# The last quarter of a weight slab's split: from GpSimd to VectorE, in every stage

## The chip, the cores and the metric

One core of one Trainium2 chip runs the whole program. The metric is device microseconds of one execution; the figure that counts is the median over several executions. The engines are named as the profile names them: PE is TensorE (PEld its weight loads), DVE is VectorE, ACT is ScalarE, POOL is GpSimd, SP is SyncE, which here issues nearly all DMAs.

## The reference, cut to what matters

256 tokens of width 1024 go through two stacks of blocks, all in float32. The first stack has two layers, each a swiglu feed forward, a mixed attention (three kinds of heads, one of them with a top-64 choice of keys by an indexer) and a second swiglu. The second stack has four layers, each a mixer (mamba2, hgrn2, gated deltanet, mamba2), a cross attention to a memory, and a convolutional glu:

```python
def swiglu(h, w1, w3, w2):
    return (jax.nn.silu(h @ w1) * (h @ w3)) @ w2
...
for i in range(DEPTH_2):
    hn = rmsnorm_2(x, ln_mix[i])
    mix = mamba2_mixer(...) | hgrn2_mixer(...) | gated_deltanet_mixer(...)
    x = x + mix
    x = x + memory_cross_attention(rmsnorm_2(x, ln_xattn[i]), rmsnorm_2(mem, ln_mem[i]), ...)
    x = x + conv_glu_ffn(rmsnorm_2(x, ln_ffn[i]), ...)
```

Every projection `h @ w` is a float32 product with some hundred tokens against a weight that is used once. The gated deltanet also solves 32 small triangular systems.

## The kernel before, in words

Weights come in slabs of 128 partitions by 2048 float32 values (1 MB, one DMA of SP each). `slab` splits a slab into a high and a low part so that three fast matmuls (high by high, high by low, low by high) give float32 accuracy: ACT writes the high part (`hi`, a rounded copy, L262), and a second engine the low part (`lo = src - hi`, L263). Tiles are named `w` (the slab as loaded, three buffers) and `wp` (its two parts, three buffers). `self.pieces` says into how many pieces the split is cut: 2 of 1024 columns in the feed forwards, 4 of 512 columns in the mixers, in the attention and in the first two steps of a swiglu. `self.share` says how many of the last pieces have their low part made by POOL in place of DVE: 1 of 4 in those stages, 3 of 4 in the triangular solve of the deltanet (`gsolve`), 0 elsewhere.

`up_block` multiplies a slab with the activations. It takes the eight contraction blocks k in turn for the slab's first 128 output columns and then again for the second 128, with three matmuls for each, 48 in all; a quarter piece of 512 columns holds two blocks k. A block of 24 matmuls so needs all four pieces. Results lie in a bank of PSUM (`up`, two of them; `acc`, four), and DVE takes them out and scales them (`scale`, L608).

Program order sets priorities: a framework's scheduler orders each engine's queue from the order in which the code records instructions and from its own idea of when each is ready. On PE the order is chained by hand (`chained`), so it is fixed. All queues run strictly in order.

In the mamba mixer a layer has 8 groups. A group takes three slabs: x (evacuated as `mps`, convolved into `mx`), B and C (evacuated as `mps` from an `acc` bank, convolved into `mbc`), and z (evacuated as `mz`). The convolutions are six fused multiply-adds of DVE each (L2016), `mm` are the decay matrices (exponentials of ACT, then times `ms` on DVE, L1430), which PE multiplies with `mxd`. POOL has other work there: masks (L1401), `mx` times a column (L1428), `my` times `mz` (L1443), a sum of squares (L1446). In the attention DVE picks the top 64 keys by repeated MAX and MATCH_REPLACE on `isc`. In `gsolve` the triangular systems are solved in 31 steps of two dependent operations each (`gyt`, a product, L1888, and `gy`, a subtraction, L1893); DVE has the columns from 20 on, POOL the columns below, while slabs of the value projection (`gpr` evacuated, `gv` convolved) go on beside it. POOL's first operation of each step is kept behind the last split that POOL was given (`self.shared`).

Of the kernel before, what the change touches and what calls it, by code (L numbers as in the profile page):

```python
# [188 lines left out]
class Net:  # L189
    def __init__(self, tc, a, out):  # L190
        self.tc, self.nc, self.a, self.out = tc, tc.nc, a, out
        self.es = ExitStack()
        pool = lambda name, bufs, **k: self.es.enter_context(tc.tile_pool(name=name, bufs=bufs, **k))
        self.cp = pool("const", 1)
        self.wp = pool("wf", 3)
        self.sp = pool("ws", 3)
        self.hp = pool("act", 1)
        self.tp = None
        self.ps = pool("ps", 2, space=PSUM)
        self.dp = pool("dram", 1, space=bass.MemoryType.DRAM)  # L200
        self.side = []
        self.pieces, self.share, self.first, self.r0 = 2, 0, False, None
        self.chain, self.linked, self.urgent, self.ready, self.beside = False, None, None, None, None
        self.shared = None
        self.table, self.used, self.loaded = None, [], None
        self.slabs, self.normed = 3, None
        self.n = 0
# [57 lines left out]
    def slab(self, src, n=2048):  # L265

        if self.ready is not None:
            parts, self.ready = self.ready, None
            return parts
        w = self.t([P, 2048], "w", pool=self.wp)[:, :n]  # L270
        if not self.first:
            self.nc.sync.dma_start(w, src)
        hi, lo = (v[:, :n] for v in self.parts([P, 2048], "w", pool=self.sp, at=0))
        m = n // self.pieces
        for k in range(0, n, m):
            if self.first:
                self.nc.sync.dma_start(w[:, k : k + m], src[:, k : k + m])
            e = self.nc.gpsimd if n - k <= self.share * m else self.nc.vector
            s = self.split(w[:, k : k + m], hi[:, k : k + m], lo[:, k : k + m], e)
            if e is self.nc.gpsimd:  # L280
                self.shared = s[1]
            if self.slabs == 2:

                for x, y in zip(s, self.normed):
                    self.after(x, y)
        self.slabs += 1
        return hi, lo
# [414 lines left out]
    def swiglu(self, l, i):  # L702
        nc, a = self.nc, self.a
        h, e = self.norm_shift(*self.mod_cols(l, 2 * i))
        w1, w3 = a["w1"][l, i], a["w3"][l, i]

        def part(s, g):
            self.pieces, self.share = (4, 1) if s < 2 else (2, 0)
            s1 = self.t([P, 2, T], "s1")
            if s == 0:  # L710
                ps = [self.acc_bank() for _ in range(4)]
# [313 lines left out]
    def attention_heads(self, l, h, qkc):  # L1025
# [50 lines left out]
        for g, ks in (  # L1076
# [14 lines left out]
        ):  # L1091
            for k in ks:
                turns.setdefault(k, []).append(g)
        self.pieces, self.share = 4, 1
        with self.chained():
            for k in range(32):
                next(units[k // 2], None)
# [1 line left out]
                    next(g, None)  # L1099
                if k in (5, 8, 11, 26, 30)[: 5 - l]:  # L1100
                    self.run_side()
        self.pieces, self.share = 2, 0

# [175 lines left out]
    def mamba(self, i):  # L1281
# [6 lines left out]
            "sums": self.dp.tile([32, T], F32, name=self.name("mad")),  # L1288
        }
        d["yh"], d["yl"] = self.parts([P, 16, T], "my", 1)  # L1290
        self.pieces, self.share = 4, 1
        with self.chained():
            groups = [self.mamba_group(ia, g, n, d) for g in range(8)]
            steps = self.mamba_steps(ia, n, d)
# [19 lines left out]
                for g in turns.get(k, []):  # L1314
                    next(g, None)
            self.residual(acc)
        self.pieces, self.share = 2, 0

    def mamba_steps(self, ia, n, d):

# [140 lines left out]
    def hgrn(self, i):  # L1461
# [21 lines left out]
        zeroed = self.t([P, 4, 512], "hz", bufs=1)  # L1483
        nc.gpsimd.memset(zeroed, 0.0)
        yh, yl = self.parts([P, 8, T], "hyy", 1)
        self.pieces, self.share = 4, 1
        with self.chained():
            pairs = [self.hgrn_pair(p, n, lb, ln1, zeroed, yh, yl) for p in range(4)]

# [18 lines left out]
                for g in turns.get(k, []):  # L1508
                    next(g)
            self.residual(acc)  # L1510
        self.pieces, self.share = 2, 0

    def hgrn_project(self, src, n, tag, bufs):

# [145 lines left out]
    def gdn(self, i):  # L1660
# [14 lines left out]
        with self.chained(), self.phase("gvalues"):  # L1675
# [3 lines left out]
            values = [self.gdn_value(n, h, vt, z) for n in range(16)]  # L1679
            half = self.gdn_halves(keys, values)  # L1680
            with self.phase("gkeys"):
                self.share = 1
                gates = self.gdn_gates(h, d)
                turns = {1: [gates], 4: [gates], 5: [gates]}
                for n in range(0, 8, 2):
                    for k, g in ((6, n), (6, n + 1), (8, n), (9, n + 1)):
                        turns.setdefault(2 * n + k, []).append(keys[g])
                for k in range(22):
                    next(half)
                    for g in turns.get(k, []):  # L1690
                        next(g, None)
            self.share = 3
            with self.phase("gsolve"):
                for k, _ in enumerate(self.gdn_solve(d)):
                    if k % 2:
                        next(half)
                for _ in range(6):
                    next(half)
            self.share = 1
            with self.phase("gcombine"):  # L1700
                pool = self.tp
                groups = [self.gdn_combine(d, q, pool) for q in range(8)]
# [5 lines left out]
                with self.phase("gheads"):  # L1708
# [15 lines left out]
                                w = self.down_slab(a["gout"][0, n // 2])  # L1724
                            self.down_step(acc, w, n % 2, y[n], n == 0, n == 15, range(2 * q, 2 * q + 2))
                    self.residual(acc)
        self.pieces, self.share = 2, 0

    def gdn_halves(self, keys, values):

# [138 lines left out]
    def gdn_solve(self, d):  # L1869
# [12 lines left out]
        for j in range(31, 0, -1):  # L1882
            for k, (e, c0, c1) in enumerate(((nc.vector, max(j, cut), 32), (nc.gpsimd, j, cut))):
                n = c1 - c0
                if n > 0:
                    sh = [P, n, j]
                    m = self.t([P, 256], f"gyt{k}", bufs=1)[:, : n * j].rearrange("p (c r) -> p c r", c=n)
                    ins = e.tensor_tensor(  # L1888
                        m, u[:, j : j + 1, 0:j].to_broadcast(sh), y[:, c0:c1, j : j + 1].to_broadcast(sh), op=OP.mult
                    )  # L1890
                    if k:
                        self.after(ins, self.shared)
                    e.tensor_tensor(y[:, c0:c1, 0:j], y[:, c0:c1, 0:j], m, op=OP.subtract)  # L1893
            yield
        for b in blocks:
# [235 lines left out]
```

## Time and profile before

| | |
|---|---|
| median of 3 executions | 3231.4 us (3229.79 to 3231.53) |
| profiled execution, its own time | 3237.62 us |
| span of the trace in it | 3235.8 us |
| busy: PE, PEld | 3113.1 us (96%), 3009.9 us (93%) |
| busy: DVE, ACT, POOL | 2407.7 us (74%), 1871.9 us (58%), 616.2 us (19%) |

Times of the trace are microseconds from the span's start. A row of the timeline merges instructions of one kind that follow one another: start, length from the first start to the last end, engine, line, operation, tiles written and read, shape, count; in square brackets is how long the engine was idle before it and what ended that. The matmuls are pipelined, so PE's busy share says little of its pace.

### The profile page before, as it was taken

The numbers are of one execution on the slowest core, as the hardware profiler recorded it, in microseconds if no ns is written. First come the engines' busy times: TensorE is split into PE (matmuls) and PEld (weight loads), VectorE is DVE, ScalarE is ACT, GpSimd is POOL, SyncE is SP. The second block draws the span as 40 slices with busy tenths as digits, with TensorE's granted clock in tenths as the row PEclk, the third lists the DMA queues.
The fourth block names the chain that finished last, engine by engine and source line by source line (L and its number), as shares of the span: only waits on it lengthen the run. The fifth ranks groups of instructions, "written<-read, shape, count | busy, mean of one in ns | idle before, by whom it ended". The sixth has DMA issues, their size and how long they took to land. (4 is left out here: it accounts for less than half of the span.)

```text
span 3235.8 us, 63172 instructions
## 1 busy us (share of the span) xinstructions
PE 3113.1 (96%) x25866; PEld 3009.9 (93%) x25866; DVE 2407.7 (74%) x4122; ACT 1871.9 (58%) x3317; POOL 616.2 (19%) x522
## 2 busy tenths in 40 slices
PE   8999999999999999999999999998799999999998
PEld 8999889999988999889999999997799999889998
DVE  6778678778777846887767677688957766897766
ACT  5554565454466545775545665476466545776644
POOL 1000222010032201443001220025512000443100
PEclk9999999999999999999999999999899999999999
DMA  8888435758843555445455345544334555445453
GB/s 277 316 302 318 169 131 209 293 214 303 296 161 118 212 194 185 160 157 186 170 194 181 131 170 183 183 155 178 118 112 156 194 207 199 164 171 182 162 192 123
DMA packets 96754, 624.85 MB, mean 193 GB/s; under 512 B 10640, under 2 KB 14800, under 8 KB 25424
## 3 DMA queue, kind: packets, MB, share of 16 engines
q1 hardware_dynamic: 96464, 620.82, 54.2%
q8 instruction: 203, 3.33, 0.4%
q14 instruction: 87, 0.71, 0.1%
HBM read 607.08 MB, written 13.70 MB: 192 GB/s over the span
## 5 line engine op out<-in xcount | busy, mean ns | idle before, releaser
L298 PE MATMUL up<-hp,wp 128*128 128x256 f32 x12360 | 1495.5, 282 | 14.9 <-DVE gpr L608 8.1
L298 PEld LDWEIGHTS up<-hp,wp 128*128 128x128 f32 x12360 | 1464.2, 191 | 28.3 <-issue 10.4
L262 ACT ACTIVATE wp<-w 128x512 fp32r<-128x512 f32 (+3 forms) x1392 | 1034.6, 787 | 699.7 <-PE acc L298 227.6
L263 DVE TENSOR_TENSOR wp<-w,wp 128x512 fp32r<-128x512 f32 (+3 forms) x1195 | 1139.9, 984 | 387.4 <-ACT wp L262 375.8
L263 POOL TENSOR_TENSOR wp<-w,wp 128x512 fp32r<-128x512 f32 (+1 forms) x197 | 282.7, 1438 | 1389.1 <-ACT wp L262 1284.5
L298 PE MATMUL acc<-gp,wp 128*128 128x256 f32 x4224 | 502.2, 279 | 0.0
L298 PEld LDWEIGHTS acc<-gp,wp 128*128 128x128 f32 x4224 | 494.7, 189 | 0.2
L455 DVE SCALAR_TENSOR_TENSOR w<-w,silu_c 128x512 f32<-128x512 f32 x288 | 191.2, 714 | 41.5 <-DMA w<-ada 41.3
L520 POOL TENSOR_TENSOR nss<-nss,nsq 128x512 f32<-128x512 f32 x38 | 52.8, 1389 | 557.3 <-ACT nsq L507 555.8
L298 PE MATMUL up<-wp,hp 128*128 128x256 f32 (+1 forms) x1056 | 145.1, 293 | 6.0 <-ACT hp L262 4.3
L298 PEld LDWEIGHTS up<-wp,hp 128*128 128x128 f32 x1056 | 134.4, 196 | 12.7 <-ACT hp L262 5.9
L298 PE MATMUL up<-mh,wp 128*128 128x256 f32 x512 | 94.5, 292 | 11.8 <-ACT wp L262 7.8
L354 ACT ACTIVATE s<-up 128x512 f32<-128x512 f32 x40 | 23.9, 598 | 125.8 <-PE up L298 125.8
L298 PE MATMUL acc<-hp,wp 128*128 128x256 f32 x768 | 95.0, 280 | 0.0
L298 PEld LDWEIGHTS up<-mh,wp 128*128 128x128 f32 x512 | 81.9, 200 | 12.9 <-ACT wp L262 8.0
L298 PE MATMUL up<-wp,mh 128*128 128x256 f32 x512 | 91.3, 280 | 2.3 <-DVE wp L263 1.9
L298 PE MATMUL acc<-xop,wp 128*128 128x256 f32 x768 | 92.9, 279 | 0.0
L298 PE MATMUL acc<-myp,wp 128*128 128x256 f32 x768 | 92.1, 280 | 0.5 <-DVE my L1442 0.5
L350 ACT ACT_TABLE_LOAD x71 | 91.1, 1283 | 1.7 <-PEq L2121 0.7
L298 PEld LDWEIGHTS acc<-myp,wp 128*128 128x128 f32 x768 | 89.6, 188 | 1.8 <-DVE my L1442 0.7
L298 PEld LDWEIGHTS acc<-xop,wp 128*128 128x128 f32 x768 | 90.3, 188 | 0.0
L298 PEld LDWEIGHTS acc<-hp,wp 128*128 128x128 f32 x768 | 90.0, 188 | 0.0
(472 smaller groups left out, 3916.5 us busy)
## 6 DMA issues: line engine op xcount, KB each, us to landing
w<-w SPq DMA_DIRECT2D x132, 1024.0 KB, 5.2
w<-ada SPq DMA_DIRECT2D x72, 1024.0 KB, 5.0
w<-min SPq DMA_DIRECT2D x48, 1024.0 KB, 4.9
w<-fg SPq DMA_DIRECT2D x44, 1024.0 KB, 4.9
w<-fu SPq DMA_DIRECT2D x44, 1024.0 KB, 4.9
w<-fd SPq DMA_DIRECT2D x44, 1024.0 KB, 4.9
w<-gin SPq DMA_DIRECT2D x24, 1024.0 KB, 5.0
w<-xv SPq DMA_DIRECT2D x16, 1024.0 KB, 6.2
```

What stands on the lines that cost most here:

```text
L262: a = self.nc.scalar.activation(hi, src, AF.Copy)
L263: return a, (engine or self.nc.vector).tensor_tensor(lo, src, hi.bitcast(F32), op=OP.subtract)
L298: self.link(self.nc.tensor.matmul(out, lhsT=lhsT, rhs=rhs, start=start, stop=stop, skip_group_check=True))
L350: self.loaded = self.nc.scalar.preload_act_table_set(name)
L354: self.used.append(self.after(self.nc.scalar.activation(out, src, func, **k), self.loaded))
L455: ins = nc.vector.scalar_tensor_tensor(c, c, 1.0, self.silu_c[:, z * 512 : z * 512 + 512], op0=OP.mult, op1=OP.mult, accum_out=sums[:, s % ...
L520: nc.gpsimd.tensor_tensor(s, s, q, op=OP.add)
```

## The change

`share` and `shared` go away. Every low part of a weight slab is made by DVE; the pieces stay as they are, and so do ACT's high parts, the DMAs and PE's order. In the solve POOL's product is no longer ordered behind a split.

```diff
@@ slab
-            e = self.nc.gpsimd if n - k <= self.share * m else self.nc.vector
-            s = self.split(w[:, k : k + m], hi[:, k : k + m], lo[:, k : k + m], e)
-            if e is self.nc.gpsimd:
-                self.shared = s[1]
+            s = self.split(w[:, k : k + m], hi[:, k : k + m], lo[:, k : k + m])
@@ swiglu
-            self.pieces, self.share = (4, 1) if s < 2 else (2, 0)
+            self.pieces = 4 if s < 2 else 2
@@ attention, mamba, hgrn (each)
-        self.pieces, self.share = 4, 1
+        self.pieces = 4
...
-        self.pieces, self.share = 2, 0
+        self.pieces = 2
@@ gdn: keys, solve, combine
-                self.share = 1
-            self.share = 3
-            self.share = 1
@@ gdn_solve
-                    ins = e.tensor_tensor(
+                    e.tensor_tensor(
                         m, u[:, j : j + 1, 0:j].to_broadcast(sh), y[:, c0:c1, j : j + 1].to_broadcast(sh), op=OP.mult
                     )
-                    if k:
-                        self.after(ins, self.shared)
```

POOL has 197 instructions fewer and DVE 197 more; PE, ACT and SP have the same instructions. Queue rows below are line, operation, tile written and tiles read with their numbers, shape, count.

First place: DVE in a middle group of the second mamba layer, from one evacuation of B and C (`mps3370`) to the next evacuation of x (`mps3392`). Slab `wp3375` belongs to z (`mz3377`), `wp3390` to the following x, `wp3396` to the following B and C, and `wp3405` to the following z. Before:

```order
L608 TENSOR_TENSOR mps3370_33039<-acc3367_32980,nr3215_31569 128x512
L263 TENSOR_TENSOR wp3390_33168<-w3389_33166,wp3390_33168 128x512 x3
L2016 SCALAR_TENSOR_TENSOR mbc3371_33041<-mps3370_33039,cols_98,mbc3371_33041 128x255 x2
L2016 SCALAR_TENSOR_TENSOR mbc3371_33041<-mps3370_33039,cols_98,mbc3371_33041 128x254 x2
L2016 SCALAR_TENSOR_TENSOR mbc3371_33041<-mps3370_33039,cols_98,mbc3371_33041 128x253 x2
L263 TENSOR_TENSOR wp3396_33244<-w3395_33242,wp3396_33244 128x512 x3
L608 TENSOR_TENSOR mz3377_33116<-up3376_33067,nr3215_31569 128x512
L263 TENSOR_TENSOR wp3405_33331<-w3404_33329,wp3405_33331 128x512
L1442 TENSOR_TENSOR my3372_33050<-acc3373_33051,mx3333_32682 128x512
L263 TENSOR_TENSOR wp3405_33331<-w3404_33329,wp3405_33331 128x512 x2
L608 TENSOR_TENSOR mps3392_33226<-up3391_33177,nr3215_31569 128x512
```

The same stretch of DVE's queue after the change:

```order
L604 TENSOR_TENSOR mps3370_33039<-acc3367_32980,nr3215_31569 128x512
L262 TENSOR_TENSOR wp3375_33058<-w3374_33056,wp3375_33058 128x512 x2
L2007 SCALAR_TENSOR_TENSOR mbc3371_33041<-mps3370_33039,cols_98,mbc3371_33041 128x255 x2
L2007 SCALAR_TENSOR_TENSOR mbc3371_33041<-mps3370_33039,cols_98,mbc3371_33041 128x254 x2
L2007 SCALAR_TENSOR_TENSOR mbc3371_33041<-mps3370_33039,cols_98,mbc3371_33041 128x253 x2
L262 TENSOR_TENSOR wp3375_33058<-w3374_33056,wp3375_33058 128x512 x2
L262 TENSOR_TENSOR wp3390_33168<-w3389_33166,wp3390_33168 128x512 x4
L262 TENSOR_TENSOR wp3396_33244<-w3395_33242,wp3396_33244 128x512 x3
L604 TENSOR_TENSOR mz3377_33116<-up3376_33067,nr3215_31569 128x512
L1438 TENSOR_TENSOR my3372_33050<-acc3373_33051,mx3333_32682 128x512
L262 TENSOR_TENSOR wp3396_33244<-w3395_33242,wp3396_33244 128x512
L604 TENSOR_TENSOR mps3392_33226<-up3391_33177,nr3215_31569 128x512
```

The last two pieces of the slab for `mz3377` now stand behind the convolution `mbc3371`; before, that slab's pieces on DVE were done a group earlier (in the rows before, the slab that follows `mz3377` is the next z, `wp3405`) and its fourth was POOL's. Slabs 1577, 1607, 1637 and 1667 of the first mamba layer and 3375, 3405 and 3435 of the second have their last two pieces moved so, and slab 3345 its last one.

Second place: DVE in the attention of the first layer, at the top-64 choice. Slab `wp523` belongs to one of the attention's input projections. Before, from its third piece on DVE to the end of the choice (its fourth was POOL's):

```order
L263 TENSOR_TENSOR wp523_5167<-w522_5165,wp523_5167 128x512
L773 TENSOR_TENSOR ropeu493_5014<-qn475_4908,consts_1050 128x128
...
L884 MATCH_REPLACE isc425_4606<-m8521_5160,isc425_4606 128x256
L882 MAX m8530_5223<-isc425_4606 128x8
L882 MAX m8531_5224<-isc425_4606 128x8
L884 MATCH_REPLACE isc425_4606<-m8530_5223,isc425_4606 128x128
L884 MATCH_REPLACE isc425_4606<-m8531_5224,isc425_4606 128x256
L888 TENSOR_SCALAR selb346_4114<-isc425_4606 128x128
L888 TENSOR_SCALAR selb346_4114<-isc425_4606 128x256
```

After, the end of the same stretch:

```order
L880 MATCH_REPLACE isc425_4606<-m8521_5160,isc425_4606 128x256
L262 TENSOR_TENSOR wp523_5167<-w522_5165,wp523_5167 128x512
L878 MAX m8530_5223<-isc425_4606 128x8
L878 MAX m8531_5224<-isc425_4606 128x8
L880 MATCH_REPLACE isc425_4606<-m8530_5223,isc425_4606 128x128
L880 MATCH_REPLACE isc425_4606<-m8531_5224,isc425_4606 128x256
L884 TENSOR_SCALAR selb346_4114<-isc425_4606 128x128
L884 TENSOR_SCALAR selb346_4114<-isc425_4606 128x256
```

The fourth piece has come to stand 15 instructions behind the third, with four passes of the choice and the rotation of `qn` in between. The second layer's attention has the same with its slab 1184.

Third place: DVE in the triangular solve, a few of its 31 steps. After the change a split stands between many of the dependent pairs; between the first step and the transposes that end the solve there are 30 splits, 8 evacuations `gpr` and 24 convolution steps `gv`, where there were 5, 5 and 17:

```order
L1881 TENSOR_TENSOR gyt02576_25831<-gu2551_25651,gy2552_25652 128x192
L262 TENSOR_TENSOR wp2608_26028<-w2607_26026,wp2608_26028 128x512
L1884 TENSOR_TENSOR gy2552_25652<-gy2552_25652,gyt02576_25831 128x8x24
L262 TENSOR_TENSOR wp2608_26028<-w2607_26026,wp2608_26028 128x512
L1881 TENSOR_TENSOR gyt02577_25834<-gu2551_25651,gy2552_25652 128x207
L262 TENSOR_TENSOR wp2608_26028<-w2607_26026,wp2608_26028 128x512
```

The three splits in these rows were POOL's before.

## Rows read from the trace of the kernel before

**Rows 1.** The page's first part: busy us, share of the span, instructions.

```profile
PE 3113.1 (96%) x25866; PEld 3009.9 (93%) x25866; DVE 2407.7 (74%) x4122; ACT 1871.9 (58%) x3317; POOL 616.2 (19%) x522
```

**Rows 2.** Groups by line, first the page's: count, busy us, mean ns, idle before.

```profile
L263 POOL TENSOR_TENSOR wp<-w,wp 128x512 fp32r<-128x512 f32 (+1 forms) x197 | 282.7, 1438 | 1389.1 <-ACT wp L262 1284.5
...
L263 DVE TENSOR_TENSOR wp<-w,wp 128x512 fp32r<-128x512 f32 x606 | 458.8, 788 | 99.6 <-ACT wp L262 88.2 <-issue 8.0 <-PE up L298 1.8
...
L2016 DVE SCALAR_TENSOR_TENSOR s<-fgs,cols,s 128x255 f32<-128x255 f32 x88 | 38.7, 478 | 2.0 <-ACT s L2014 2.0
...
L2016 DVE SCALAR_TENSOR_TENSOR mbc<-mps,cols,mbc 128x255 f32<-128x255 f32 x32 | 27.4, 894 | 0.0
```

**Rows 3.** Windows: stretch, PE, PEld, DVE, ACT, POOL busy, granted clock, DMA.

```profile
324.00:570.00 246.00, 236.85 (x1771) 214.67 (x1770) 187.27 (x428) 153.98 (x341) 62.95 (x55) 0.98 0.48 171
...
1770.00:1900.00 130.00, 129.15 (x1101) 125.53 (x1101) 86.95 (x162) 83.79 (x157) 34.13 (x24) 1.00 0.44 156
...
2255.00:2323.00 68.00, 46.07 (x345) 44.59 (x343) 66.46 (x105) 24.89 (x55) 43.33 (x60) 0.89 0.34 121
...
2750.00:2960.00 210.00, 195.90 (x1579) 183.53 (x1578) 178.99 (x297) 154.24 (x299) 89.92 (x71) 0.97 0.46 161
```

**Rows 4.** Windows of line 263 alone: DVE busy (count), POOL busy (count).

```profile
324.00:570.00 246.00, 86.73 (x118) 32.12 (x23) 0.98 0.48 171
...
1770.00:1900.00 130.00, 46.06 (x62) 20.58 (x15) 1.00 0.44 156
...
2255.00:2323.00 68.00, 5.58 (x7) 28.46 (x21) 0.89 0.34 121
2750.00:2960.00 210.00, 72.94 (x101) 44.12 (x29) 0.97 0.46 161
```

**Rows 5.** Timeline of the triangular solve.

```profile
2267.13 1.31 POOL L263 TENSOR_TENSOR wp<-w,wp 128x512 fp32r<-128x512 f32 x1
2267.22 1.50 DVE L2016 SCALAR_TENSOR_TENSOR gv<-gpr,cols,gv 128x255 f32<-128x255 f32 x1
```

**Rows 6.** Timeline of one mamba group in the second layer: DVE, then POOL, then PE.

```profile
2853.60 1.93 DVE L1430 TENSOR_TENSOR mm<-mm,ms 128x384 f32<-128x384 f32 x4
...
2858.00 3.48 DVE L2016 SCALAR_TENSOR_TENSOR mbc<-mps,cols,mbc 128x255 f32<-128x255 f32 x6
2861.41 1.88 DVE L263 TENSOR_TENSOR wp<-w,wp 128x512 fp32r<-128x512 f32 x3
...
2869.51 0.69 DVE L608 TENSOR_TENSOR mps<-up,nr 128x512 f32<-128x512 f32 x1 [3.22 <-PE up L298]
2870.25 1.95 DVE L1455 SCALAR_TENSOR_TENSOR hy<-my,cols,rstd 128x256 f32<-128x256 f32 x2
...
2872.72 1.67 DVE L263 TENSOR_TENSOR myp<-hy,myp 128x256 fp32r<-128x256 f32 x2
2874.31 2.44 DVE L2016 SCALAR_TENSOR_TENSOR mx<-mps,cols,mx 128x255 f32<-128x255 f32 x6
2876.68 1.94 DVE L1430 TENSOR_TENSOR mm<-mm,ms 128x384 f32<-128x384 f32 x4
...
2858.12 1.51 POOL L263 TENSOR_TENSOR wp<-w,wp 128x512 fp32r<-128x512 f32 x1 [1.79 <-ACT wp L262]
...
2854.19 2.00 PE L298 MATMUL acc<-mm,mxd 128*64 128x256 f32 x8 [2.25 <-DVE mm L1430]
2856.13 6.44 PE L298 MATMUL up<-hp,wp 128*128 128x256 f32 x48
...
2863.74 5.74 PE L298 MATMUL up<-hp,wp 128*128 128x256 f32 x48
```

**Rows 7.** Timeline of the first attention, at the end of the top-64 choice.

```profile
442.53 1.29 POOL L263 TENSOR_TENSOR wp<-w,wp 128x512 fp32r<-128x512 f32 x1 [2.98 <-ACT wp L262]
...
447.46 2.99 PE L298 MATMUL up<-hp,wp 128*128 128x256 f32 x24
451.58 0.70 PE L298 MATMUL ms<-nsq,consts 128*128 128x256 f32 x2 [1.14 <-ACT nsq L984]
...
451.41 0.61 DVE L882 MAX8 m<-isc 128x8 f32<-128x128 f32 x2
```

More of the change, by code (lines that the diff above doesn't have):

```diff
@@ L201, in __init__ @@
         self.side = []
-        self.pieces, self.share, self.first, self.r0 = 2, 0, False, None
+        self.pieces, self.first, self.r0 = 2, False, None
         self.chain, self.linked, self.urgent, self.ready, self.beside = False, None, None, None, None
-        self.shared = None
         self.table, self.used, self.loaded = None, [], None
@@ L1290, in mamba @@
         d["yh"], d["yl"] = self.parts([P, 16, T], "my", 1)
-        self.pieces, self.share = 4, 1
+        self.pieces = 4
         with self.chained():
@@ L1316, in mamba @@
             self.residual(acc)
-        self.pieces, self.share = 2, 0
+        self.pieces = 2
     def mamba_steps(self, ia, n, d):
@@ L1485, in hgrn @@
         yh, yl = self.parts([P, 8, T], "hyy", 1)
-        self.pieces, self.share = 4, 1
+        self.pieces = 4
         with self.chained():
@@ L1510, in hgrn @@
             self.residual(acc)
-        self.pieces, self.share = 2, 0
+        self.pieces = 2
     def hgrn_project(self, src, n, tag, bufs):
@@ L1726, in gdn @@
                     self.residual(acc)
-        self.pieces, self.share = 2, 0
+        self.pieces = 2
     def gdn_halves(self, keys, values):
```

## The prediction

> **What bounds the kernel now.** The engine totals come first: PE is busy for 3113.1 us of the span, 96%, DVE for 74%, POOL for 19% [rows 1]. As a mean that leaves DVE 828 us of room, and 197 more splits look free. A mean over stages doesn't decide it, so the next view is the windows [rows 3], with the split's own line beside them [rows 4]. The reader is to see three kinds of stage. In hgrn2 PE is busy for 129.15 of 130 us and DVE for 87: whatever DVE gets there, PE has its next slab. In the solve it is the reverse: DVE 66.46 of 68 us, PE 46.07 for 345 matmuls at a granted clock of 0.89, so DVE sets the time. The attention (DVE 187.3 of 246, clock 0.98) and mamba (DVE 179 of 210, PE 196, clock 0.97) lie between: PE is the bound with gaps, and a gap is DVE being late at one place. One mamba gap stands in the timeline: PE waits 2.25 us for `mm` of DVE [rows 6].
>
> **What goes and what comes.** The order shows the move done in full: 197 splits fewer on POOL, 197 more on DVE, so that the change doing nothing is ruled out. On POOL they took 282.7 us at 1438 ns each, and POOL was mostly waiting for ACT's high part ahead of them [rows 2]; no stage had POOL as its bound, so this time is worth nothing by itself. On DVE a split's mean is 788 ns [rows 2], but three in a row take 1.88 us [rows 6]: 0.63 each, the next beginning before the last has ended. 197 × 0.63 = 124 us of work added to DVE at most (eleven of the moved pieces are smaller).
>
> **What DVE gets back.** The trace shows that a DVE instruction beside a POOL split can stand still. In the solve `gv` 128x255 began 0.09 us behind a POOL split and took 1.50 us, ending 0.19 us after the split's 2268.44 [rows 5]; the same shape takes 0.478 as a mean over 88 [rows 2]. That is 1.02 us for one hit. The convolution `mbc` has a mean of 894 ns where `s<-fgs`, the same operation and shape, has 478: 32 × 0.416 = 13.3 us, or 0.83 for each of the 16 mamba groups, and in the group shown `mbc` x6 took 3.48 against 2.44 for `mx` x6, with POOL's split at 2858.12 beside it [rows 2, 6]: 1.04 again. A split that meets DVE waiting, or a DVE operation that it doesn't disturb, gives back nothing. So a moved split costs DVE 0.63 and returns 0 to 1.04; DVE's time is even when 61 of 100 splits hit. Bounds for DVE's busy time: all hit, 124 − 205 = −81 us; none, +124. With DVE 74% busy as a mean and nearer 85 to 98% in mamba and the solve, where a hit is likeliest, I take about six hits in ten, so DVE's total stays about even. What is left is the order: the work that comes back is an average, the late piece is at a place.
>
> The Trainium skill says the same of the cause and more of the size (SBUF — State Buffer, section Who interferes with whom): a DVE instruction with two SBUF inputs contends with a GpSimd instruction that reads SBUF, and the second of them blocks fully until the first is done. The hit of [rows 5] agrees. Were every split to block DVE for its whole length, DVE would get back 283 us for 124 by that rule (an estimate, from the 282.7 of [rows 2]). [Rows 6] show 1.04 for a split of 1.51, so the sum goes by the rows.
>
> **Mamba, where order costs.** Before, the z slab's last piece was POOL's and early; DVE's three were done a group ahead. Now its last two stand behind `mbc` in the first `order` place, for seven slabs of the two layers, and in an eighth one piece does: 8 of 16 groups. Worked on the group shown [rows 6], counted from `mm` at 2853.60: `mm` 1.93, then an evacuation and two splits (0.6 + 1.26), so `mbc` begins at about 3.8. It now takes 2.44: 6.2. Two splits more end at 7.5. PE needs the last piece for 6 matmuls of the first half and then for the 24 of the second: 30 at 0.12 (5.74 us for 48) = 3.6, end at 11.1. In the trace `up` ended at 2862.57, which is 8.97 after `mm`. So z's block ends 2.1 later, and nothing in front of PE covers it, as PE's order is fixed. Some of it comes back in the same period of 23.08 us (`mm` at 2853.60 and 2876.68): the run from `mps` to the next `mm` lies on the path too (2869.51 to 2876.68), and at most one hit of 1.0 is in it; three splits fewer or more move in this period. I take 0.8 back: +1.3 × 8 = +10. The other eight groups keep their order and get about 0.2 each: −2. Mamba: +8. Bounds: if the returned hits count in full and the late pieces are covered, −1.04 × 16 = −17; if nothing comes back, 8 × 2.1 + 8 × 1.26 = +27.
>
> **Attention.** POOL had the fourth piece of the slab at 442.53 to 443.82, and `up` began at 447.46 [rows 7]. Now DVE has it after the MATCH_REPLACE that comes just before the last pair of MAX, at 451.41: ready at about 452.1. Of the first block 18 matmuls can be done by then, six are left, 0.7: 452.8. PE went on to `ms` at 451.58, since it waited there anyhow for ACT (1.14); so the loss is 1.2, and two layers have it: +2.4. For the other 44 of the 46 splits here DVE's idle quarter (59 of 246 us) is the cover; without it, 12 more us. Bounds 0 (the choice runs earlier by as much as its hits are gone) to +10 (the piece delays the choice and both blocks).
>
> **Solve.** DVE is full, so each split counts: 21 × 0.63 = +13 [rows 4]. Of POOL's 28.46 us of splits there, with DVE busy for 98% of the time, most hit: 0.75 × 21 × 1.03 = −16. Net −3. The pairs `gyt`, `gy` depend on each other, and a split between them fills the time between; POOL's half of the steps no longer waits for splits. Bounds 13 − 22 = −9 to +6 (a third of them hit).
>
> **The rest.** hgrn2, the keys, the feed forwards' first slabs: PE 129 of 130 us [rows 3], DVE with 43 us of room in 130 for 15 × 0.63 = 9: nothing. If that cover were gone, 9 us.
>
> **Sum.** +8 + 2.4 − 3 = about +8 on the profiled execution's 3237.6: 3245 to 3246. That execution lies 6.2 above the median, so in terms of the median 3231.4 + 8 = about **3240**.
>
> **Rivals.** (a) *DVE becomes faster where it counts.* The freed `mbc`, `mx`, `gv` act on the path in all 16 groups and in the solve, and the late pieces are covered: −17 − 3 − 1, so 3210. For it: `mbc` is 0.83 a group longer than it need be, and PE waits for `mm`. Against: z's last piece comes after `mbc` in half of the groups, whatever `mbc` takes. It decides if `mbc` begins 2 us earlier than I have it, which needs the hits of the stretch before it to be two, not one. By the Trainium skill's rule above, this is what should happen. (b) *No change.* The late pieces end up in waits that are there: DVE waits 3.22 for PE ahead of `mps` [rows 6], PE for ACT in the attention. The +10 halves, the −2 and −3 stay: 3231 to 3236. For it: PE is 96% busy and most changes off it vanish. Against: DVE's wait for PE is not PE's wait, and the order of PE is fixed. (c) *DVE is the new bound of mamba and the solve*, with hits fewer than 4 in 10: +27 + 6 + 5, so 3270. Against: `mbc`'s 894.
>
> **Chances.** Slower as forecast 0.40, (c) 0.06, (b) 0.33, (a) 0.21. A measurement of this kernel tells about 0.2%, 6.5 us, from no change. The forecast of +8 lies near that bound, so some of its chance lies within it and some of (b) above: slower 0.45, same 0.34, faster 0.21. The likeliest case's own range is 3234 to 3248. The range holds most of (a) and leaves (c)'s end out: 3215 to 3262.
>
> **What would show it.** Right: `mbc`'s mean falls from 894 to about 480, DVE's split from 788 to about 700; DVE's busy total stays within 40 us of 2408; in mamba PE's `up` of 48 that follows the `mm` product waits for DVE's line of the split, about 2 us, in eight groups, where it had no such wait; in the attention `up` of 24 before `ms` stretches from 2.99 to about 5; the solve's window stays within some 5 us of 68. Wrong: `mm` to `mm` in mamba falls below 23.08 (then (a) is right), DVE's busy total falls by over 60 (hits are the rule), or rises by over 80 (they were rare), or PE waits for DVE in hgrn2, which I hold covered.

## The result: 43 us faster

The changed kernel takes 3188.3 us (3183.95 to 3192.29, 4 runs) against 3231.5 (3229.79 to 3238.45): a ratio of 0.9862, with a 95% interval of 0.9826 to 0.9898. The forecast was 3240, and the range began at 3215. The profiled execution has a span of 3188.0 us, 47.8 less than that of before. The page's first part answers to [rows 1], the groups by line and shape to [rows 2]:

```profile
PE 3085.4 (97%) x25866; PEld 2983.9 (94%) x25866; DVE 2396.7 (75%) x4319; ACT 1872.3 (59%) x3317; POOL 348.8 (11%) x325
```

```profile
L262 DVE TENSOR_TENSOR wp<-w,wp 128x512 fp32r<-128x512 f32 x792 | 550.3, 730 | 91.0 <-ACT wp L261 88.1 <-PE up L294 1.8
...
L2007 DVE SCALAR_TENSOR_TENSOR mbc<-mps,cols,mbc 128x255 f32<-128x255 f32 x32 | 14.6, 485 | 0.0
```

DVE has 197 instructions more and is busy 11 us less. `mbc` has fallen from 894 to 485 ns, the split from 788 to 730. So the stalls that POOL's splits had caused gave back about what the splits cost.

The windows of [rows 3], between the same matmuls (PE's order is the same in both kernels, so the k-th matmul marks the same place), and the span with its mean granted clock:

```profile
325.50:563.80 238.30, 232.84 (x1772) 212.00 (x1772) 185.88 (x455) 154.13 (x341) 32.68 (x32) 0.99 0.50 178
...
2217.30:2296.20 78.90, 62.83 (x535) 61.22 (x533) 76.86 (x154) 39.58 (x88) 17.64 (x38) 0.91 0.42 145
2700.30:2905.40 205.10, 191.71 (x1579) 178.91 (x1578) 175.69 (x326) 154.74 (x299) 45.75 (x42) 1.00 0.46 165
```

```profile
core 0: 3188.0 us, clock 0.992
```

The attention has lost 7.8 us and the second mamba layer 5.0; the solve with its transposes, up to the matmul that stood at 2345 before, takes 78.9 us where it took 89.9. The granted clock of the whole is 0.992 where it was 0.984: about 104 us at the lower level before, 51 after (twice the missing part of the clock, times the span). A microsecond at half clock costs at most half a microsecond, so this is up to 26 us of the 47.8. It is more than the usual difference: the kernel before was granted 0.983 to 0.990 in its executions on record, 0.987 on average, which against 0.992 makes some 16 us.

What PE waited for in the second mamba layer, from the view of waits (us, times, longest), first before, then after:

```profile
PE acc L298 <- DVE mm L1430: 11.0, 7, 2.4
PE ms L319 <- DVE mdd L1333: 1.8, 1, 1.8
PE up L298 <- DVE mm L1430: 1.3, 1, 1.3
```

```profile
PE up L294 <- DVE wp L262: 10.1, 7, 1.9
PE acc L294 <- DVE mm L1426: 2.3, 5, 0.7
PE ms L315 <- DVE mdd L1329: 0.8, 1, 0.8
```

The late z pieces are there: the seven waits lie in four groups of the layer and come to 1.9 to 2.8 us a group, where about 2 was forecast. What was not forecast: 10.0 us of waits for `mm` went. All waits of the layer together hardly fell, from 14.1 to 13.2 us, and the groups did not fare alike. The first `mm` of the layer's first group and of its last, before and then after (the fourth group's stand at 2853.60 in [rows 6] and at 2795.62 below):

```profile
2783.07 0.56 DVE L1430 TENSOR_TENSOR mm<-mm,ms 128x384 f32<-128x384 f32 x1 [0.19 <-PE ms L298]
...
2945.08 1.93 DVE L1430 TENSOR_TENSOR mm<-mm,ms 128x384 f32<-128x384 f32 x4
```

```profile
2732.53 0.54 DVE L1426 TENSOR_TENSOR mm<-mm,ms 128x384 f32<-128x384 f32 x1
...
2890.09 1.93 DVE L1426 TENSOR_TENSOR mm<-mm,ms 128x384 f32<-128x384 f32 x4
```

The first three periods from `mm` to `mm` took 70.5 us before and take 63.1; the last four, those with a late piece, took 91.5 and take 94.5. In the first mamba layer it is 72.6 and 64.0, then 91.3 and 96.1. One group with a late piece in the timeline of the changed kernel, DVE and then PE, against [rows 6]:

```profile
2795.62 1.94 DVE L1426 TENSOR_TENSOR mm<-mm,ms 128x384 f32<-128x384 f32 x4
2797.48 0.68 DVE L604 TENSOR_TENSOR mps<-acc,nr 128x512 f32<-128x512 f32 x1
2798.08 1.28 DVE L262 TENSOR_TENSOR wp<-w,wp 128x512 fp32r<-128x512 f32 x2
2799.28 2.44 DVE L2007 SCALAR_TENSOR_TENSOR mbc<-mps,cols,mbc 128x255 f32<-128x255 f32 x6
2801.65 4.29 DVE L262 TENSOR_TENSOR wp<-w,wp 128x512 fp32r<-128x512 f32 x7
...
2796.22 1.33 PE L294 MATMUL acc<-mm,mxd 128*64 128x256 f32 x8 [0.65 <-DVE mm L1426]
2797.48 2.99 PE L294 MATMUL up<-hp,wp 128*128 128x256 f32 x20
2802.38 3.45 PE L294 MATMUL up<-hp,wp 128*128 128x256 f32 x28 [1.92 <-DVE wp L262]
```

`mbc` x6 takes 2.44 where it took 3.48, the z block waits 1.92 for its piece and ends at 2805.83, 10.2 after `mm` (11.1 was forecast, 9.0 before). But PE's wait for `mm` is 0.65 where it was 2.25. Ahead of the 2.25, two of the six `mx` had stood beside a split of POOL:

```profile
2849.15 2.28 DVE L2016 SCALAR_TENSOR_TENSOR mx<-mps,cols,mx 128x255 f32<-128x255 f32 x2
2848.91 1.47 POOL L263 TENSOR_TENSOR wp<-w,wp 128x512 fp32r<-128x512 f32 x1
```

In the changed kernel all six take 2.82. In the five groups of the layer where DVE has the same operations from `mps` to `mm` in both kernels, that way took 7.8 us on average and takes 6.2; half of the difference is in the operations, the other half is idle time that went too.

Behind that wait for `mm` the clock was lower as well. Windows of the kernel before, from the matmuls ahead of the wait, through those right behind it, to those after them; then of the changed kernel, through its wait for the z piece:

```profile
2849.70:2853.40 3.70, 2.25 (x20) 2.05 (x19) 3.70 (x8) 2.95 (x4) 1.45 (x2) 1.00 0.51 157
2854.20:2857.40 3.20, 3.20 (x14) 2.35 (x15) 3.20 (x6) 3.20 (x8) 1.27 (x1) 0.51 0.08 31
2858.00:2862.40 4.40, 4.40 (x41) 4.40 (x40) 4.40 (x9) 0.63 (x1) 1.51 (x1) 1.00 0.66 238
```

```profile
2796.20:2802.40 6.20, 4.12 (x29) 3.26 (x29) 6.20 (x14) 4.92 (x10) 0.00 (x0) 1.00 0.00 0
2802.40:2805.80 3.40, 3.40 (x29) 3.40 (x30) 3.40 (x6) 0.05 (x1) 0.00 (x0) 1.00 0.72 236
```

Behind the wait for `mm` the clock was granted at 0.51, the lower of the two levels (1.2 GHz), for some 3 us: 14 matmuls in 3.2 us where 41 follow in 4.4. In the changed kernel it stays at 1.00 through the wait for the piece. Not every wait is followed by a lower clock: three of the layer's eight waits for `mm` were, but a wait of 2.37 us at 2900.11 was not; in the changed kernel's first mamba layer one of the seven waits for the piece was.

In the solve, the same steps of before and after, DVE's columns at width 228:

```profile
2286.14 1.49 DVE L1888 TENSOR_TENSOR gyt<-gu,gy 128x228 f32<-128x228 f32 x1
2287.66 1.38 DVE L1893 TENSOR_TENSOR gy<-gy,gyt 128x228 f32<-128x228 f32 x1
```

```profile
2247.44 0.38 DVE L1881 TENSOR_TENSOR gyt<-gu,gy 128x228 f32<-128x228 f32 x1
2247.75 0.68 DVE L604 TENSOR_TENSOR gpr<-up,nr 128x512 f32<-128x512 f32 x1
2248.35 0.38 DVE L1884 TENSOR_TENSOR gy<-gy,gyt 128x228 f32<-128x228 f32 x1
```

1.49 and 1.38 have become 0.38 and 0.38, and an evacuation fits between.

### The profile page after: what moved, and what is told of

It reads as the page before. It is cut to its first block, busy times and chain, and to the rows that moved or that the text cites. A ratio compares the mean times of both kernels' runs of the same rounds, so it can differ in the third digit from the quotient of the medians.

```text
span 3188.0 us, 62851 instructions
## 1 busy us (share of the span) xinstructions
PE 3085.4 (97%) x25866; PEld 2983.9 (94%) x25866; DVE 2396.7 (75%) x4319; ACT 1872.3 (59%) x3317; POOL 348.8 (11%) x325
## 5 line engine op out<-in xcount | busy, mean ns | idle before, releaser
L262 DVE TENSOR_TENSOR wp<-w,wp 128x512 fp32r<-128x512 f32 (+3 forms) x1392 | 1232.1, 918 | 373.5 <-ACT wp L261 364.9
L294 PEld LDWEIGHTS up<-hp,wp 128*128 128x128 f32 x12360 | 1449.3, 189 | 51.6 <-DVE wp L262 37.3
L451 DVE SCALAR_TENSOR_TENSOR w<-w,silu_c 128x512 f32<-128x512 f32 x288 | 184.5, 690 | 48.0 <-DMA w<-ada 47.8
L294 PEld LDWEIGHTS up<-wp,hp 128*128 128x128 f32 x1056 | 131.8, 193 | 11.1 <-ACT hp L261 4.3
L294 PEld LDWEIGHTS up<-wp,mh 128*128 128x128 f32 x512 | 79.5, 191 | 7.4 <-DVE wp L262 4.5
L604 DVE TENSOR_TENSOR fgs<-up,nr 128x512 f32<-128x512 f32 x44 | 30.3, 689 | 73.7 <-PE up L294 73.7
```

Of the source, the lines that this page charges most:

```text
L262: return a, (engine or self.nc.vector).tensor_tensor(lo, src, hi.bitcast(F32), op=OP.subtract)
L294: self.link(self.nc.tensor.matmul(out, lhsT=lhsT, rhs=rhs, start=start, stop=stop, skip_group_check=True))
L451: ins = nc.vector.scalar_tensor_tensor(c, c, 1.0, self.silu_c[:, z * 512 : z * 512 + 512], op0=OP.mult, op1=OP.mult, accum_out=sums[:, s % ...
L604: self.nc.vector.tensor_tensor(out, ps.rearrange("p (b t) -> p b t", b=n), r[:, :T].unsqueeze(1).to_broadcast([P, n, T]), op=OP.mult)
```

## The experiments

Lengths of seven stretches in each run's profile, between the same two matmuls (before, they lie at 324:570, 891:1134, 1296:1500, 2110:2255, 2255:2345, 2345:2470 and 2750:2960), in us. "Keys" and "combine" are the deltanet ahead of and behind its solve. A number in bold is of a stretch whose splits are all DVE's with nothing put in their place on POOL.

| kernel | attention 1 | attention 2 | mamba 1 | keys | solve | combine | mamba 2 |
|---|---|---|---|---|---|---|---|
| before | 246.1 | 243.0 | 204.1 | 145.1 | 89.9 | 125.2 | 210.1 |
| changed | **238.2** | **237.2** | **201.3** | **138.6** | **78.9** | **118.3** | **205.1** |
| changed, once more | **239.3** | **237.3** | **202.1** | **138.7** | **80.9** | **119.9** | **204.8** |
| solve alone | 243.6 | 242.7 | 200.3 | 145.4 | **79.1** | 126.1 | 208.0 |
| all but the solve | **238.1** | **237.2** | **201.9** | **140.8** | 88.6 | **118.4** | **205.1** |
| mamba alone | 244.7 | 243.0 | **201.2** | 145.9 | 88.9 | 125.9 | **206.8** |
| attention alone | **241.5** | **238.4** | 201.9 | 145.7 | 88.9 | 126.4 | 209.1 |
| POOL's twin | 249.0 | 247.5 | 203.0 | 145.8 | 97.4 | 118.7 | 207.8 |
| POOL's fills | 242.6 | 238.9 | 201.1 | 140.6 | 87.2 | 118.3 | 208.3 |
| extra on DVE | 246.7 | 246.7 | 201.3 | 146.4 | 97.9 | 125.1 | 213.9 |
| early z | **239.7** | **236.3** | **191.6** | **138.7** | **80.9** | **119.8** | **197.6** |

Within a column, plain rows of before's kind (POOL's twin, POOL's fills and the extra on DVE aside) and bold rows keep apart, but for mamba 1 (200.3 to 204.1 against 201.2 to 202.1); in attention 1 and mamba 2 they do so by 2.1 and 1.2 us, no more than they scatter. The mamba columns of the last row have that kernel's own edit in them. Read so, the change is worth between 5 and 6 us in each attention, 6 in the keys, 9 in the solve, 7 in the combine, 4 in the second mamba layer and none that shows in the first: 37 in all, by the means. The 7.8 us read above for attention 1 are not all the change's. The kernel before ran it mostly at the slower of the two paces of the last section (the median step between matmuls that follow closely is 117 ns there), the changed kernel at the faster (114); "solve alone", with attention 1 as before, ran it at 114 too and has 243.6, which is 2.5 less.

The time that a stretch loses can be a wait of PE or a lower clock. Over the seven stretches, in the first two rows, PE's waits come to 79.3 us and 60.7, and the time at the lower level to 90.3 us and 37.5, of which half is 26.4 us less. Added up, this is 45.0 of the 45.9 us that these stretches lost (a rough sum, as the pace counts too); so by this count the clock is the larger part. In the combine it is all there is: PE's waits are 5.1 us before and 5.0 after. The combine before, a part of it, and the combine after:

```profile
2345.00:2470.20 125.20, 119.68 (x1222) 113.21 (x1217) 72.38 (x155) 78.99 (x209) 28.18 (x29) 0.94 0.36 127
2369.60:2383.20 13.60, 13.13 (x87) 11.56 (x85) 3.66 (x10) 4.68 (x13) 0.00 (x0) 0.50 0.00 0
```

```profile
2296.20:2414.50 118.30, 113.08 (x1223) 107.19 (x1218) 75.77 (x163) 78.34 (x208) 16.99 (x21) 1.00 0.40 142
```

The combine has 14 to 17 us at the lower level in all rows where POOL makes splits for it, and none or 3.4 in all others, POOL's twin and fills among them. So there the gain does not come from POOL's reads; what ties the clock to the splits was not found.

**The solve alone, and all but the solve.**

```diff
@@ gdn (of the kernel before)
-            self.share = 3
+            self.share = 0
```

> Only the triangular solve has its splits moved from POOL to DVE; all other stages keep their POOL quarter. Theory A (the gain is local to the stages whose DVE queue was full): the stretch from 2255 to 2323 of the kernel before shortens by 17 us as in the changed kernel, and the whole by 15 to 19: about 3214. Theory B (most of the 43 us is a state of TensorE, its granted clock and its pace per matmul, that moves with any edit): the stretch shortens by less than 8 us and the total lies anywhere between 3190 and 3235 without matching a stage.

Ratio 0.9973 (0.9945 to 1.0001), 3221.6 us. The other half, with `share` 0 in all stages but that one:

> All stages but the solve have their splits on DVE; the solve keeps three of four pieces on POOL and its ordering. Theory A: the remainder of the gain, 43 - 17 = 26 us, so about 3205. Theory B: not additive, the sum of this gain and that of the run with the solve alone misses 43 by more than 10 us.

Ratio 0.9874 (0.9826 to 0.9922). As gains these are 9 and 41 us; together 50 us, against 45 by the changed kernel's ratio, so the parts add within their intervals. Beyond the scatter, the stretches shorten where they are changed and nowhere else: theory A. The stretch that was named, 2255 to 2323, does shorten by 17 us, from 68.1 to 50.8, but the solve's part is 9 to 11: the 17 had been read at an earlier matmul, and some of it is given back right behind, where PE waits once, in the changed kernel too, for a split that stands behind the four transposes:

```profile
2285.80 1.22 PE L294 MATMUL up<-hp,wp 128*128 128x256 f32 x4 [6.83 <-DVE wp L262]
```

**Mamba alone, attention alone.** The same edit in one stage's line (`4, 1` to `4, 0`).

> Only the two mamba layers have their splits on DVE. Theory A: each layer loses its seven waits of PE for the mm product (11 us) and gets seven waits for a late z piece (10 us), and the stretches of half clock that followed the mm waits go: -3 in the first layer, -5 in the second, about 3223. The forecast on record had +8 for the two layers: about 3240.

Ratio 0.9999 (0.9973 to 1.0025), which is 0 us, from −9 to +8: nothing that the times can tell, and the −8 of theory A and the +8 on record both lie near its ends. In the profile the second layer is 3.3 us shorter than before's and 1.2 to 2.3 shorter than the other plain rows (5 was expected), the first within its scatter. So +8 is not seen in the stretches.

> Only the two attentions have their 46 splits on DVE. Theory A (a held-up DVE operation lies on the chains that PE waits for, while the added splits fill DVE's idle time): the two attentions lose some 5 to 6 us each in waits and half clock, as in the changed kernel, about 3219 beside a kernel before at 3231. The forecast on record had +2.4.

Ratio 0.9982 (0.9956 to 1.0007), 6 us where 12 were expected; the two stretches are 4.6 us shorter each, a little under theory A's 5 to 6.

**The contention by itself.** DVE has all splits, the solve's products are no longer ordered behind them, as in the changed kernel, and POOL does a twin for each split that it lost:

```diff
@@ slab (share and pieces as in the kernel before)
+            s = self.split(w[:, k : k + m], hi[:, k : k + m], lo[:, k : k + m])
             if e is self.nc.gpsimd:
-                self.shared = s[1]
+                x = hi[:, k : k + m].bitcast(F32)
+                e.tensor_tensor(w[:, k : k + m], x, x, op=OP.subtract)
```

> The changed kernel, where for each of the 197 moved splits POOL also does a subtraction of the same size, of a finished high part from itself, into the weight slab that the split has just read; nobody uses what it writes, but the slab's buffer comes free after it. Theory A (a POOL operation that reads beside a DVE operation of two inputs holds it up by about 1 us): most of the gain goes, the mean of DVE's split of 512 columns rises from about 0.7 to 0.79 or more, and the total is 3225 to 3260. Theory C (the gain is from where the low parts stand and when they come, POOL having been a late supplier): the total stays at 3185 to 3200.

Ratio 1.0076 (1.0052 to 1.0100), 3258.5 us. The page and the split's group:

```profile
PE 3109.7 (96%) x25866; PEld 3004.6 (92%) x25866; DVE 2471.7 (76%) x4319; ACT 1870.8 (57%) x3317; POOL 608.3 (19%) x522
...
L263 DVE TENSOR_TENSOR wp<-w,wp 128x512 fp32r<-128x512 f32 x792 | 581.3, 770 | 87.6 <-ACT wp L262 82.1 <-issue 3.0 <-PE up L299 1.8
```

The split's mean is 770 ns, not quite the 790 expected. DVE's queue holds the same work as in the changed kernel and is busy 75 us longer; the time is 69 us longer (1.0076 less 0.9862, of 3230). Three fills in place of the subtraction keep POOL as busy, and free the slab as late, without a read:

```diff
-                e.tensor_tensor(w[:, k : k + m], x, x, op=OP.subtract)
+                for _ in range(3):
+                    e.memset(w[:, k : k + m], 0.0)
```

> As the run with POOL's twin subtraction, but with three fills of the same 128x512 columns with zeros in place of each subtraction: POOL is occupied for about as long (a fill of 128x1024 takes 0.95 us, three of 512 about 1.5) and frees the slab's buffer as late, but reads nothing. If DVE is held up by POOL's reads (theory A), the 70 us that the twin cost go and the time is that of the changed kernel, 3185 to 3200, with a mean of about 730 ns for DVE's split. If it was POOL's occupied queue (its other operations late) or the late buffer, the time stays near the twin's 3258, at least over 3225.

Ratio 0.9942 (0.9912 to 0.9973), between both expectations.

```profile
PE 3091.8 (96%) x25866; PEld 2990.0 (93%) x25866; DVE 2405.3 (75%) x4319; ACT 1874.4 (58%) x3317; POOL 642.7 (20%) x916
...
L263 DVE TENSOR_TENSOR wp<-w,wp 128x512 fp32r<-128x512 f32 x792 | 545.6, 726 | 90.0 <-ACT wp L262 87.2 <-PE up L299 1.8
```

DVE is back at 2405 and 726 ns, with POOL busier than ever: what holds DVE up is that POOL reads. This agrees with the Trainium skill, SBUF — State Buffer, section Who interferes with whom: a DVE operation with two inputs in SBUF is in conflict with a GpSimd operation that reads SBUF, not with one that only writes. Of the twin's 69 us some 43 are the reads; 26 stay with the fills. 6 to 8 of these lie in the solve, where POOL's steps stand ahead of the fills in its queue and the slab's buffer comes free late (ACT waits 15.1 us for slabs there, 6.6 in the changed kernel); how the rest divides between late buffers and POOL's other work was not taken apart.

By stretch, the twin is longer than the fills by 6 and 9 us in the attentions, 5 in the keys and 10 in the solve, and by no more than 2 in the combine and the two mamba layers. In mamba its reads fell elsewhere than those of POOL's splits had: `mbc` has a mean of 535 ns and not 894, and PE's waits for `mm` in the whole program are 7.9 us (22.7 before, 5.6 in the changed kernel). So the pair shows what POOL's reads cost in attention, keys and solve; that they caused the waits for `mm` rests on the timeline of before.

**The added work by itself.** POOL keeps its splits, and DVE does one operation more for each:

```diff
@@ slab (of the kernel before)
             if e is self.nc.gpsimd:
                 self.shared = s[1]
+                x = hi[:, k : k + m].bitcast(F32)
+                self.nc.vector.reduce_max(self.t([P, 1], "more", bufs=1), x, axis=mybir.AxisListType.X)
```

> The kernel before, POOL's splits kept, and for each of them one operation of the same length more on DVE (a maximum over the 512 columns of the high part, which nobody uses), at its place in the program: the debit of the change without its credit. Theory A (what is added on DVE falls into its idle time, except behind the late pieces): 197 x 0.63 = 124 us of work cost less than 25 us, 3235 to 3260 beside a kernel before at 3231, and most of that in the solve, where DVE is full. The reasoning on record (added work and returned work weigh the same): DVE's busy total of 2408 rises by some 120 and the time by 50 or more.

Ratio 1.0102 (1.0069 to 1.0136), 33 us.

```profile
PE 3114.0 (96%) x25866; PEld 3010.4 (92%) x25866; DVE 2508.4 (77%) x4319; ACT 1872.7 (58%) x3317; POOL 602.6 (19%) x522
```

DVE is busy 100.7 us longer, 0.51 for each operation, and the program 33: 0.33 us of time for each us of work added (0.22 to 0.44), more than theory A allowed, less than the reasoning on record. A us of stall costs about twice that: 43 of time for the 66 of DVE that lie between the twin and the fills, 0.65 (0.46 to 0.85 by the two ratios' intervals). The added operation is one that nobody waits for; a moved split can also be late for PE, which the next run prices. From this kernel to the changed one DVE loses 112 us and the program 78 (1.0102 less 0.9862, of 3230). Both roads, extra work on the kernel before and POOL's twin on the changed one, end near 3258.

**The late piece.** In each mamba group the z slab is recorded ahead of the convolution of B and C, and `halves` takes it as it is:

```diff
@@ mamba_group
             y = self.t([P, 2, T], ("mx", "mbc")[s])
+            wz = self.up_slab(src(2)) if s else None
...
-        z = yield from self.halves(src(2), n, "mz", 2)
+        z = yield from self.halves(src(2), n, "mz", 2, w=wz)
```

> The changed kernel, with the z slab of each mamba group recorded ahead of the convolution of B and C, so that all its splits stand before that convolution on DVE. If the late z piece is what PE waits for in the mamba layers (10 us in each), these waits go and the two layers become 8 to 20 us shorter: 3168 to 3182. If the wait only moves (the four splits push the convolution, the decay product and so `acc` back by up to 2.5 us in a group), PE waits for the mm product instead and the total stays within 5 us of the changed kernel.

Ratio 0.9801 (0.9767 to 0.9834), 3175.1 us; the two layers are 9.7 and 7.5 us shorter than in the changed kernel. PE's waits in the second layer:

```profile
PE acc L294 <- DVE mm L1427: 2.6, 6, 0.8
PE up L294 <- DVE wp L262: 2.5, 3, 0.8
```

The waits for the piece fell from 10.1 to 2.5 us and did not move to `mm`. So the cost of the late piece on record was real (17 us for both layers); it was outweighed.

**Further off POOL.** Four products of the mixers and the attention (44 operations) put on DVE, on top of the early z:

> The kernel with the early z slab, and four products that are left on POOL (the gate products of the three mixers and the norm gain of the attention's queries, 44 operations of 0.7 to 2.1 us) put on DVE too. Theory A says that what holds for splits holds for them: each costs DVE 0.4 to 0.7 us and gives back about 1 us where it met a DVE operation, and its own result comes 0.5 to 1.5 us earlier; 5 to 15 us faster than the kernel with the early z slab alone. If DVE's queue in the mamba layers (86% busy) is now the bound, the layers become longer instead.

Ratio 0.9799 (0.9769 to 0.9829): the same as with the early z alone. The gain of 5 to 15 us is not there: either these products meet little on DVE, or what they give back is not waited for; this was not taken apart. With the 32 splits of the cross attention and 30 products of the norms as well:

> The kernel with the early z slab and the four products on DVE, and 32 splits of the cross attention's keys and values (1.5 to 1.8 us each on POOL) and 30 products of the norms (1.0 us each) on DVE too. If the lesson of the splits holds wherever POOL reads beside DVE, 5 to 10 us less than that kernel's 3172. If the norms and the cross attention are bound by DVE or by DMA at those places, no gain: 3168 to 3180.

Ratio 0.9755 (0.9713 to 0.9797), 3143.6 us, 14 less by the ratios, more than the 5 to 10 expected, though the two intervals overlap; and with the last eight kinds of products:

> The kernel with an early z slab and less on POOL (3144), with POOL's eight remaining kinds of two-input products put on DVE as well, all but the solve's columns and the norms' sums. If every POOL read beside DVE costs more than the work itself, another 5 to 15 us: 3130 to 3140. If what is left on POOL meets DVE idle, or DVE's queue is now what PE waits for, no gain or a loss: 3140 to 3160.

Ratio 0.9686 (0.9658 to 0.9715), 3125.0 us, the best of all, and 22 less by the ratios where 5 to 15 were expected. POOL is busy for 61 us, and DVE, with 424 instructions more than before, for less than before:

```profile
PE 3071.6 (98%) x25866; PEld 2978.1 (95%) x25866; DVE 2397.6 (76%) x4546; ACT 1869.6 (60%) x3317; POOL 61.0 (2%) x98
...
L262 DVE TENSOR_TENSOR wp<-w,wp 128x512 fp32r<-128x512 f32 x792 | 517.0, 686 | 90.0 <-ACT wp L261 87.0 <-PE up L294 1.8 <-PE acc L294 0.3
```

**The spread of one program.**

> The changed kernel once more, as it is, for the spread of one program. Theory B (TensorE's pace per matmul takes one of two values in a stage, 113 or 118 ns, by chance and not by the edit): the stages with few waits (the feed forwards) show the other of the two values in at least two of the places where the first execution had one of them. If the pace belongs to the program, every stage repeats its value and the total lies within 3 us of 3188.

Ratio 0.9861 (0.9829 to 0.9893), the same as the first time. Neither expectation holds whole: nearly every stage repeated its pace, and one, the last feed forward, took the other value (last section).

## Why the prediction was wrong

**The balance on DVE was right.** Its busy total was to stay within 40 us of 2408 and is 2397. The page's group of all splits of DVE, before and after, is 92.2 us longer for 197 more; all else on DVE is so 103.2 us shorter:

```profile
L263 DVE TENSOR_TENSOR wp<-w,wp 128x512 fp32r<-128x512 f32 (+3 forms) x1195 | 1139.9, 984 | 387.4 <-ACT wp L262 375.8
```

```profile
L262 DVE TENSOR_TENSOR wp<-w,wp 128x512 fp32r<-128x512 f32 (+3 forms) x1392 | 1232.1, 918 | 373.5 <-ACT wp L261 364.9
```

With the extra operation as the measure of a split's work, 0.51 us of work for each split and 0.57 of returned stall (112 over 197) stand where the forecast had 0.63, and 1.03 for six splits in ten, 0.62.

**The step that failed** is the one that turned this balance into time: "What is left is the order: the work that comes back is an average, the late piece is at a place". The debit of the late piece was about right. The credit was the term that was mis-sized: 0.2 us for each mamba group without a late piece, none for the attentions, the keys and the combine, and no term at all for the clock. The runs show the credit at places too, on the way to what PE waits for (`mx` ahead of `mm`, `gv`, `gyt`), and stages gain that were put at nothing: 7 to 9 us in three periods of each mamba layer, 5 to 6 in each attention, 6 in the keys, 7 in the combine. A us of stall was worth about twice a us of added work (0.65 and 0.33), and up to 26 of the 47.8 us between the two profiles came by the clock. Why a stall is so much dearer is only argued: the scheduler placed each split by its own idea of time, and no stall is in it.

**The terms.** By the table's means the stretches lost 37 us where 8 more were forecast; of the 45 between, 12 are mamba's, 13 the attentions', 6 the solve's and 13 those of the keys and the combine. Mamba, +8: a period with a late piece is 1.2 us longer in the first layer and 0.8 in the second, where +1.3 was forecast, but the other three are 8.5 and 7.4 us shorter together. Measured 0 to −4. Attention, +2.4: no credit was counted at all, and the piece was not late. The rows that answer to [rows 7], PE and the piece on DVE:

```profile
445.02 3.25 PE L294 MATMUL up<-hp,wp 128*128 128x256 f32 x24
448.11 0.59 PE L294 MATMUL ms<-nsq,consts 128*128 128x256 f32 x2
...
446.80 0.68 DVE L262 TENSOR_TENSOR wp<-w,wp 128x512 fp32r<-128x512 f32 x1
```

The piece came 2.5 us after `up` began where 4.6 had been worked out, since the choice ahead of it ran earlier too; `up` took 3.25 for 2.99. Measured −5 to −6 in each layer. The solve, −3: measured −9, at the bound of −9; three more slabs' evacuations and more of the convolutions had room in it, which the order had shown. The window of 68 us, which was to stay within 5, has become 51.2, of which a part is lost again right behind:

```profile
2217.30:2268.50 51.20, 41.96 (x345) 40.68 (x344) 51.13 (x109) 25.68 (x58) 17.64 (x38) 0.93 0.40 139
```

The rest, nothing: right for hgrn2 (130.0 us and 130.1), wrong for the keys and the combine of the deltanet, −6 and −7, for which no rows had been read.

**What was not in the sum** is the clock: behind the wait of 2.25 us some 3 us ran at half clock, and in the combine nearly 14 us with hardly a wait. The mean rose from 0.984 to 0.992, up to 26 of the 47.8 us between the profiles. A part of that follows waits that went; for the combine the cause stays open.

**The rivals.** (a), DVE faster where it counts, was the nearest, with 0.21 and −21, but not as it was put. Its late pieces were to be covered, and four groups of each layer wait for them; its sign, `mm` to `mm` below 23.08, did not come in the group shown (2795.62 to 2819.11, 23.49) but in the groups without a late piece. It decided not where the forecast said (two hits ahead of `mbc`) but on the path to `mm`. It was sized by mamba and the solve alone and without the clock, so even its 3210 was short of 3188. The Trainium skill's rule that stood beside it, by which the second of two that meet waits for the whole of the first, speaks for the side that won; the trace has 0.57 us a split as a mean, not the 1.44 that a full block of every split would give, and a mean cannot tell a shorter block from splits that met nothing.

## What to carry to other kernels

Where GpSimd reads beside a VectorE queue that a matmul waits for, compare the busy total of VectorE with the sum of its operations at their undisturbed length; the difference is work that GpSimd costs, and here it was as large as the work that it took over. Count that credit at the operation that the matmul waits for, stage by stage, and the debit where the queue has room; two terms of one size on the engine need not be of one size in time. Read the granted clock of each stage before and after: a stage can gain by it alone. And look for the piece that comes late after such a move: recording one slab earlier gave another 13 us in the medians, 20 by the ratios.

## What was not expected of the hardware

In these profiles PE's pace at a granted clock of 1.00 has two values, and a stage keeps one of them for a hundred us and more. The same stretch of the same program, the last feed forward of the changed kernel, in its first and its second profile:

```profile
3102.59 11.47 PE L294 MATMUL up<-hp,wp 128*128 128x256 f32 x96
...
3119.55 11.47 PE L294 MATMUL up<-hp,wp 128*128 128x256 f32 x96
```

```profile
3101.86 11.04 PE L294 MATMUL up<-hp,wp 128*128 128x256 f32 x96
...
3118.18 11.04 PE L294 MATMUL up<-hp,wp 128*128 128x256 f32 x96
```

The starts, with the 48 matmuls of `acc` between, are 16.96 and 16.32 us apart: 117.8 and 113.3 ns for each of the 144, with no wait between them. Over that stage it is 6 us, which is about what two executions of one program differ by, and more than some of the terms above. Between the two profiles of the result such changes of pace nearly cancel: the first feed forward behind the attention went to the faster value, later stages to the slower. What chooses the value stays open.
